# Where the weight operands stand in SBUF, relative to what streams past them

## The chip, the cores and the metric

One core of a Trainium2 chip runs the kernel. The metric is the device time of one execution in microseconds (us). On-chip memory is SBUF (128 partitions) and PSUM, where matmul results land. TensorE does matmuls in two kinds of instruction that the profile shows apart: PEld loads a weight operand into the array, PE streams the other operand (the moving one) past it. PEld of the next matmul runs beside PE of the present one. DVE and ACT are the engines for elementwise work, POOL and SP mostly start DMAs.

## The reference

Two layers, each: a gated feed-forward block (SwiGLU, inner width 2816), a mixer of three branches (RWKV-7, gated linear attention, attention into a memory of 256 rows) that are gated and merged, and a second feed-forward block. 512 tokens, width 1024, float32.

```python
for l in range(DEPTH):
    x = x + 0.5 * swiglu_ffn(rmsnorm(x, ffn1_norm[l]), ffn1_w_in[l], ffn1_w_out[l])
    h = rmsnorm(x, mix_norm[l])
    u_rwkv, u_gla, u_xa, u_gate = split_cols(h @ w_in[l], ...)
    ...
    merged = jnp.einsum('bsjc,jcd,bsjd->bsd', branches, w_branch[l], gates)
    x = x + merged @ w_out[l]
    x = x + 0.5 * swiglu_ffn(rmsnorm(x, ffn2_norm[l]), ffn2_w_in[l], ffn2_w_out[l])
return rmsnorm(x, final_norm)
```

## The kernel before

Every large product runs in the type float32r, on operands that are split in two: `hi` is the value rounded by ACT to float32r, `lo` is the rest, subtracted by DVE (`split`, L721). A product is then three matmuls: the moving hi and the moving lo past the weight's hi, and the moving hi past the weight's lo.

The feed-forward blocks and the mixer's last product cut each product into seven smaller ones (`seven`, L897, a Strassen-like scheme on blocks). A job of `seven` has seven parts, each with a weight of its own, four from two-chunk pieces and three from narrow ones; `part` (L841) runs one part: per 128 rows the two matmuls past hi, and then the ones past lo. All these matmuls stream 256 columns (128x256 in the profile). There are 10,708 of them. The mixer's projections (`proj`, `product`, `mm3`) and the first few columns of each feed-forward block (`whole`, L985) stream 512 columns (128x512); there are about 4,060 of those. About 1,530 float32 matmuls in the mixer are smaller.

`piece` (L834) makes the split weight of one or two parts. A raw tile with two chunks (`wraw`, `q`) goes to tiles `whi`/`wlo` in the pool `wp`; a narrow one, with one chunk (`e[:, 0:1]`, `e[:, 1:2]`, `d`), goes to tiles `fhi`/`flo` in the pool of the stage (`ffn`, or `mg` in the mixer's last product). Each of these four names is a ring of two buffers. In a profile, `hi` and `lo` are the names of all of them.

The moving operands stand in the pool `keep` (`xhi`, `xlo`, `n`, `t`, `yh`, `yl`) or in the pool of the stage (`mh`, `ml`, `xrh`, `xrl`). SBUF is given out pool after pool: `const`, `keep`, `wp`, `nrm`, and then the pool of the stage. Modulo 256 bytes that gives, in the built program:

| operands | pool | byte modulo 256 |
|---|---|---|
| moving xhi, xlo, n, t, yh, yl | keep | 128 |
| moving mh, ml, xrh, xrl | ffn, mg | 192 |
| weights of pieces with two chunks, and of `wide` | wp | 128 |
| weights of narrow pieces | ffn, mg | 192 |

So the distance of a weight from what streams past it (weight minus moving, modulo 256) is 0, 64 or 192, by the part. In the up-projection (moving from `keep`) parts with two-chunk pieces have 0 and narrow ones 64; in the down-projection (moving from `ffn`) two-chunk pieces have 192 and narrow ones 0. The mixer's 512-wide products have 0, those of `whole` 192.

Nothing here is issued in the order of the code: all operations are recorded, a planner (`plan`, `run`, `choose`) simulates the engines with a table of costs, and the program is issued in the order that it found. The planner knows that a buffer of a ring can be written again only when all instructions on the tile that held it before are done. All instructions have the one line of the recorder's call (L316), so the profile is read by tiles.

Of the kernel before, what the change touches and what calls it, by code (L numbers as in the profile page):

```python
# [11 lines left out]
F32 = mybir.dt.float32  # L12
F32R = mybir.dt.float32r
# [6 lines left out]
P = 128  # L20
T = 512
# [7 lines left out]
HALVES = slice(0, H), slice(H, T)  # L29
NWHOLE = [[4, 4], [4, 4]]  # L30
NWARM = 12
NQ = 5
EPS = 1e-6
LN_EPS = 64e-5
# [63 lines left out]
class Tile:  # L98
    def __init__(self, pool, shape, dt, name, tag, bufs):
        self.pool, self.shape, self.dt, self.name, self.tag, self.bufs = pool, shape, dt, name, tag, bufs  # L100
        self.real, self.users, self.writes, self.reads, self.runs = None, [], [], [], ([], [])
        self.before, self.gone, self.free = (), None, False
# [491 lines left out]
class Net:  # L594
    def __init__(self, ctx, tc, I):
        self.nc, self.I = Recorder(tc), I
        self.const = self.pool("const", 1)
        self.keep = self.pool("keep", 1)
        self.wp = self.pool("wp", 2)
        self.nrm = self.pool("nrm", 1)  # L600
        self.psb = self.pool("psb", 3, space=PSUM)
        self.pss = self.pool("pss", 1, space=PSUM)
        self.psy = self.pool("psy", 1, space=PSUM)
        self.dram = self.pool("dram", 1, space=bass.MemoryType.DRAM)
# [24 lines left out]
    def setup(self):  # L629
        nc, I = self.nc, self.I  # L630
        self.pars = [self.const.tile([P, NPAR], F32, name=f"par{l}", tag=f"par{l}") for l in range(L)]
        self.par = self.pars[0]
        nc.scalar.dma_start(out=self.par, in_=I["par"][0])
        self.one = self.const.tile([P, 1], F32, name="one", tag="one")
        nc.vector.memset(self.one, 1.0)
        ps = self.psy.tile([P, T], F32, name="ps_y", tag="y", free=True)
        for _ in range(NWARM):
            nc.tensor.matmul(ps[:, :P], self.one.to_broadcast([P, P]), self.one.to_broadcast([P, P]), start=True, stop=True)
        self.turn = 0
        self.xs = self.keep.tile([P, KD, T], F32, name="x", tag="x")  # L640
        self.x = [self.xs[:, k, :] for k in range(KD)]
        for k in range(KD):
            nc.sync.dma_start(out=self.x[k], in_=I["x"][k * P:(k + 1) * P, :])
        self.cst = self.const.tile([P, P], F32, name="cst", tag="cst")
        nc.sync.dma_start(out=self.cst, in_=I["cst"][:, :P])
        for l in range(1, L):
            nc.sync.dma_start(out=self.pars[l], in_=I["par"][l])
        self.eps = self.const.tile([P, 2], F32, name="eps", tag="eps")
        nc.vector.memset(self.eps[:, 0:1], EPS)
        nc.vector.memset(self.eps[:, 1:2], LN_EPS)  # L650

        self.sums, self.par7 = {}, False
        self.yd = self.dram.tile([3, P, T], F32, name="yd", tag="yd")
        self.yx = self.dram.tile([4, P, T], F32, name="yx", tag="yx")
        self.xd = self.dram.tile([KD, P, T], F32, name="xd", tag="xd")
        self.vd = [self.dram.tile([4, P, T], F32, name=f"vd{l}", tag=f"vd{l}") for l in range(L)]
# [127 lines left out]
    def raw_in(self, pool, norm):  # L784

        hi, lo = (pool.tile([P, 7, T], F32R, name="xr" + c, tag=f"m01{c}", bufs=1) for c in "hl")
        r = pool.tile([P, 2, T], F32R, name="xr", tag="q", bufs=NQ)
        xs = [(hi[:, k, :], lo[:, k, :]) for k in range(7)] + [(r[:, 0], r[:, 1])]
# [44 lines left out]

    def piece(self, pool, raw):  # L834

        p, tags = (self.wp, ("whi", "wlo")) if raw.shape[1] == 2 else (pool, ("fhi", "flo"))
        hi, lo = (p.tile(list(raw.shape), F32R, name=t[1:], tag=t, bufs=2) for t in tags)
        self.split(hi, lo, raw)
        return [(hi[:, c, :], lo[:, c, :]) for c in range(raw.shape[1])]

# [56 lines left out]
    def seven(self, pool, src, n, ops, evict, clear=False):  # L897
# [7 lines left out]
        def begin():  # L905
# [3 lines left out]
            nc.gpsimd.dma_start(out=a[:, 1], in_=w[:, 3], accum_op=ALU.add)  # L909
            q = ring("q", NQ)  # L910
            nc.sync.dma_start(out=q[:, 1], in_=w[:, 2])
            e = ring("q", NQ)
            nc.sync.dma_start(out=e[:, 0], in_=w[:, 1])
# [871 lines left out]
    def mem_norm(self, pool):  # L1785

        nc, I = self.nc, self.I
        mt = [pool.tile([P, 4, NMEM], F32, name="m", tag="q", bufs=NQ) for _ in range(2)]
        mt = [t[:, k, :] for t in mt for k in range(4)]
# [118 lines left out]
```

## Time and profile before

| | |
|---|---|
| median of 3 runs | 2533.76 us (2532.69 to 2534.31) |
| the profiled execution | 2534.68 us |
| its span on the core | 2532.7 us |
| DMA over the span | 358.02 MB, mean 141 GB/s |
| ACT, POOL busy | 1466.9 us (58%), 241.2 us (10%) |

The profile's page gives busy times, the chain of work that ended last and the costliest groups. The timeline view lists instructions in order of their start (start, length, engine, output tile<-moving tile,weight tile, count). A matmul's listed length contains its way through the array, so it is longer than the distance from its start to the start of the next; this distance is what a matmul costs where PE never waits. Below, "distance" means this, start to start.

### The profile page before, as it was taken

To read this page: it belongs to the slowest core of one execution; us is meant where nothing else is said; L and a number is where in the kernel's file an instruction comes from. 1 tells how busy PE (TensorE), PEld (TensorE's weight loads), DVE (VectorE), ACT (ScalarE), POOL (GpSimd) and SP (SyncE) were. 2 spreads that over 40 slices of the span, in tenths; PEclk is the share of its full clock that TensorE was granted. 3 is DMA by queue.
4 is the path that set the end of the run, shared out by engine and by line. 5 is a ranking of instruction groups with operands and counts; after the bars stand their busy time and mean duration, and the time that the engine had idled before them with its cause. 6 is when DMAs were issued, how large, how long until landed. Compare 5 with 4: busy or idle time off the path is not lost.

```text
span 2532.7 us, 47197 instructions
## 1 busy us (share of the span) xinstructions
PE 2506.4 (99%) x17636; PEld 2270.3 (90%) x17636; DVE 2100.5 (83%) x4218; ACT 1466.9 (58%) x2660; POOL 241.2 (10%) x362
## 2 busy tenths in 40 slices
PE   9999999999999999999999999999999999999998
PEld 8999988888788799999989999887887888899998
DVE  8988885778888689888899888866888877898878
ACT  6665666564544456565665656664745444565655
POOL 1111100000000001111112111000000000011110
PEclk9999999999999999999999999999999999999999
DMA  7777762422222456877558777523222225468774
GB/s 199 194 197 189 165 190 76 125 73 69 70 83 74 141 159 150 204 186 184 143 143 203 187 184 170 176 88 101 84 72 88 67 77 171 134 162 205 188 180 105
DMA packets 163668, 358.02 MB, mean 141 GB/s; under 512 B 18256, under 2 KB 38160, under 8 KB 163440
## 3 DMA queue, kind: packets, MB, share of 16 engines
q1 hardware_dynamic: 125344, 288.87, 37.8%
q0 software_dynamic: 36864, 65.03, 16.2%
q8 instruction: 139, 2.28, 0.4%
q10 hardware_dynamic: 1232, 1.11, 0.1%
q14 instruction: 89, 0.73, 0.1%
HBM read 342.88 MB, written 12.06 MB: 140 GB/s over the span
## 4 chain that ended last, share of the span: by engine, by line
PE 85%; DVE 8%; DMA 3%; ACT 2%; issue 2%; SPq 0%; DVEq 0%; ACTq 0%; POOLq 0%
PE ps_b L316 40%; PE ps_i L316 25%; PE ps_f L316 10%; PE ps_c L316 9%; PE ps_y L316 1%; DVE wlo L316 1%; DVE lo L316 1%; DVE x L316 1%; DMA q<-in_ffn_out_dram 1%; ACT whi L316 1%; DMA wraw<-in_w_out_dram 0%; DVE ml L316 0%; DMA wraw<-in_ffn_in_dram 0%; ACT hi L316 0%; DMA q<-in_ffn_in_dram 0%
## 5 line engine op out<-in xcount | busy, mean ns | idle before, releaser
L316 ACT ACTIVATE hi<-q 128x512 fp32r<-128x512 f32 (+3 forms) x384 | 288.9, 756 | 204.8 <-PE ps_i L316 69.6
L316 DVE TENSOR_TENSOR lo<-q,hi 128x512 fp32r<-128x512 f32 (+3 forms) x384 | 321.6, 840 | 43.5 <-ACT hi L316 43.1
L316 PE MATMUL ps_b<-xhi,whi 128*128 128x512 f32 (+1 forms) x880 | 353.7, 402 | 0.2 <-DVE rk_r L316 0.2
L316 PE MATMUL ps_b<-xlo,whi 128*128 128x512 f32 (+1 forms) x880 | 352.9, 401 | 0.1
L316 PE MATMUL ps_b<-xhi,wlo 128*128 128x512 f32 x864 | 347.2, 402 | 0.6 <-DVE wlo L316 0.6
L316 DVE TENSOR_TENSOR wlo<-wraw,whi 128x1024 fp32r<-128x1024 f32 (+1 forms) x172 | 183.7, 1069 | 75.2 <-ACT whi L316 71.0
L316 ACT ACTIVATE whi<-wraw 128x1024 fp32r<-128x1024 f32 (+1 forms) x174 | 161.7, 929 | 130.0 <-PE ps_b L316 100.1
L316 DVE TENSOR_TENSOR lo<-wraw,hi 128x1024 fp32r<-128x1024 f32 (+2 forms) x162 | 191.5, 1182 | 48.5 <-ACT hi L316 46.5
L316 ACT ACTIVATE hi<-wraw 128x1024 fp32r<-128x1024 f32 (+2 forms) x162 | 166.3, 1026 | 106.1 <-PE ps_i L316 41.0
L316 PEld LDWEIGHTS ps_b<-xlo,whi 128*128 128x128 f32 (+1 forms) x880 | 164.1, 187 | 35.6 <-DVE xlo L316 2.5
L316 PEld LDWEIGHTS ps_b<-xhi,whi 128*128 128x128 f32 (+1 forms) x880 | 164.4, 187 | 33.6 <-issue 1.2
L316 PEld LDWEIGHTS ps_b<-xhi,wlo 128*128 128x128 f32 x864 | 162.7, 188 | 32.9 <-DVE wlo L316 2.4
L316 PE MATMUL ps_i<-mh,hi 128*128 128x256 f32 x628 | 157.1, 283 | 4.3 <-ACT hi L316 2.6
L316 PE MATMUL ps_i<-ml,hi 128*128 128x256 f32 x624 | 154.8, 281 | 0.0
L316 PE MATMUL ps_b<-xlo,hi 128*128 128x256 f32 x576 | 144.3, 283 | 0.0
L316 PE MATMUL ps_b<-xhi,hi 128*128 128x256 f32 x576 | 144.3, 283 | 0.0
L316 PEld LDWEIGHTS ps_i<-mh,hi 128*128 128x128 f32 x628 | 119.1, 190 | 5.9 <-ACT hi L316 3.2
L316 PEld LDWEIGHTS ps_i<-ml,hi 128*128 128x128 f32 x624 | 118.1, 190 | 0.0
L316 PEld LDWEIGHTS ps_b<-xhi,hi 128*128 128x128 f32 x576 | 110.5, 192 | 0.2
L316 PEld LDWEIGHTS ps_b<-xlo,hi 128*128 128x128 f32 x576 | 110.4, 192 | 0.2
L316 DVE TENSOR_TENSOR q<-q 128x512 f32<-128x512 f32 (+1 forms) x128 | 85.5, 668 | 22.9 <-DMA q<-in_ffn_in_dram 19.0
L316 ACT ACT_TABLE_LOAD x71 | 91.1, 1283 | 18.9 <-DVE gc L316 10.8
(416 smaller groups left out, 7021.4 us busy)
## 6 DMA issues: line engine op xcount, KB each, us to landing
wraw<-in_w_main_dram SPq DMA_DIRECT2D x108, 512.0 KB, 3.6
wraw<-in_ffn_in_dram SPq DMA_DIRECT2D x102, 512.0 KB, 4.6
q<-in_ffn_in_dram SPq DMA_DIRECT2D x144, 256.0 KB, 4.5
d<-in_ffn_in_dram SPq DMA_DIRECT2D x72, 256.0 KB, 4.2
q<-in_ffn_in_dram POOLq DMA_DIRECT2D x72, 256.0 KB, 6.0
wraw<-in_ffn_in_dram POOLq DMA_DIRECT2D x72, 256.0 KB, 5.2
wraw<-in_ffn_out_dram SPq DMA_DIRECT2D x32, 512.0 KB, 4.4
q<-in_ffn_out_dram SPq DMA_DIRECT2D x64, 256.0 KB, 3.7
```

Source lines behind the costliest of these rows:

```text
L316: return getattr(getattr(self.tc.nc, engine), what)(*(f(v) for v in a), **{n: f(v) for n, v in k.items()})
```

## The change

A tile of 48 floats (192 bytes) in a pool of its own, between `keep` and `wp`, moves `wp` and everything behind it by 192 bytes. A narrow piece no longer has a tile for hi and one for lo, but one tile `hl` of 64 + 2 x 512 floats, in which hi begins at 192 bytes and lo 2048 bytes behind it.

```diff
+SHIFT = 48
...
         self.keep = self.pool("keep", 1)
+        self.shift = self.pool("shift", 1)
         self.wp = self.pool("wp", 2)
...
+        nc.gpsimd.memset(self.shift.tile([P, SHIFT], F32, name="shift", tag="shift"), 0.0)
...
     def piece(self, pool, raw):
 
-        p, tags = (self.wp, ("whi", "wlo")) if raw.shape[1] == 2 else (pool, ("fhi", "flo"))
-        hi, lo = (p.tile(list(raw.shape), F32R, name=t[1:], tag=t, bufs=2) for t in tags)
+        if raw.shape[1] == 2:
+            hi, lo = (self.wp.tile(list(raw.shape), F32R, name=t[1:], tag=t, bufs=2) for t in ("whi", "wlo"))
+        else:
+            n = raw.shape[2]
+            f = pool.tile([P, 64 + 2 * T], F32R, name="hl", tag="fhl", bufs=2)
+            hi, lo = (f[:, SHIFT + i * T:SHIFT + i * T + n].rearrange("p (c t) -> p c t", c=1) for i in range(2))
         self.split(hi, lo, raw)
```

In the built program the moving operands now stand at 128 (`keep` and `ffn`, `mg` alike) and all split weights of these products at 64: the distance is 192 for 10,599 of the pairs of neighbouring 256-wide matmuls (before: 0 for 5,589, 64 for 2,587, 192 for 2,489) and for 3,580 of the 512-wide ones (before: 0 for 2,896, 192 for 776).

The shared tile also changes what the planner knows: hi and lo of a narrow piece come free together, when the last matmul past lo is done, where hi came free a few matmuls earlier. The table of costs is the same, but the planned order moves with it. ACT in the up-projection of the first feed-forward block, before; `fm<-ps`, `ft<-ft` and `mh<-fm` belong to the results of the running job, `hi<-q` are the two narrow pieces `e`, and `hi<-q 128x1024` is the two-chunk piece of the next job:

```order
L316 ACTIVATE fm<-ps_c 128x256
L316 ACTIVATE hi<-q 128x512 x2
L316 ACTIVATE ft<-ft 128x256
L316 ACTIVATE mh<-fm 128x256 x2
L316 ACTIVATE ft<-ps_i 128x256
L316 ACTIVATE hi<-q 128x1024
```

The same engine at the same place of a job, now:

```order
L317 ACTIVATE fm<-ps_c 128x256
L317 ACTIVATE hl<-q 128x512
L317 ACTIVATE ft<-ft 128x256
L317 ACTIVATE hl<-q 128x512
L317 ACTIVATE mh<-fm 128x256 x2
L317 ACTIVATE ft<-ps_i 128x256
```

The rounding of the second narrow piece stands behind the job's Silu (`ft<-ft`) instead of ahead of it. DVE at the same place of a job, before (`lo<-q` 128x512 are the two narrow pieces, `ft<-ps_f` and the two `fm` are results of the job):

```order
L316 TENSOR_TENSOR lo<-wraw,hi 128x1024
L316 TENSOR_TENSOR lo<-q,hi 128x512
L316 TENSOR_TENSOR ft<-ps_f,ft 128x256
L316 SCALAR_TENSOR_TENSOR fm<-ps_i,ft 128x256
L316 TENSOR_TENSOR lo<-q,hi 128x512
L316 SCALAR_TENSOR_TENSOR fm<-fm,ft 128x256
```

DVE there, now:

```order
L317 TENSOR_TENSOR lo<-wraw,hi 128x1024
L317 TENSOR_TENSOR ft<-ps_f,ft 128x256
L317 TENSOR_TENSOR hl<-q,hl 128x512
L317 SCALAR_TENSOR_TENSOR fm<-fm,ft 128x256
L317 SCALAR_TENSOR_TENSOR fm<-ps_i,ft 128x256
L317 TENSOR_TENSOR s_2271<-fm 128x256
L317 TENSOR_TENSOR hl<-q,hl 128x512
```

Both subtractions of narrow pieces moved behind one or two results of the running job. The first matmul past a narrow piece still waits for ACT's hi alone, and the first one past its lo for DVE. The number of instructions is the same but for one memset of POOL at the start.

## The prediction

> **What bounds the kernel now.** I read the page first, then the groups by shape, then the timeline of PE.
>
> ```profile
> span 2532.7 us, 47197 instructions
> PE 2506.4 (99%) x17636; PEld 2270.3 (90%) x17636; DVE 2100.5 (83%) x4218; ACT 1466.9 (58%) x2660; POOL 241.2 (10%) x362
> PEclk9999999999999999999999999999999999999999
> PE 85%; DVE 8%; DMA 3%; ACT 2%; issue 2%; SPq 0%; DVEq 0%; ACTq 0%; POOLq 0%
> ```
>
> PE is busy for 99% of the span, holds 85% of the chain that ended last, and its granted clock is full in all 40 slices. So the kernel is bound by the rate at which PE starts matmuls, and the only thing that the change can win is a shorter distance between starts. The groups say where the distance differs:
>
> ```profile
> L316 PE MATMUL ps_b<-xhi,hi 128*128 128x256 f32 x576 | 144.3, 283 | 0.0
> L316 PE MATMUL ps_i<-t,hi 128*128 128x256 f32 x576 | 79.7, 281 | 0.6 <-ACT ft L316 0.6
> L316 PE MATMUL ps_b<-mh,hi 128*128 128x256 f32 x416 | 100.6, 278 | 0.0
> ```
>
> These are the same matmuls in shape. The first has its weight at distance 0 from what streams, the second at 64, the third at 192, and the means fall from 283 to 281 to 278 ns. Addresses do go with time. The timeline shows what is behind the means. At distance 0:
>
> ```profile
> 303.56 0.28 PE L316 MATMUL ps_b<-xhi,hi 128*128 128x256 f32 x1
> ...
> 305.00 1.12 PE L316 MATMUL ps_f<-n,hi 128*128 128x256 f32 x8
> ```
>
> Twelve matmuls lie between these starts (eight past hi, four past lo): 1.44 us / 12 = 120.0 ns. At distance 192, 48 matmuls in a row:
>
> ```profile
> 2143.58 0.28 PE L316 MATMUL ps_b<-mh,hi 128*128 128x256 f32 x1
> ...
> 2149.23 0.32 PE L316 MATMUL ps_i<-ml,hi 128*128 128x256 f32 x1
> ```
>
> 5.65 us / 48 = 117.7 ns. And once more distance 192, around a stall:
>
> ```profile
> 318.99 0.28 PE L316 MATMUL ps_b<-ml,hi 128*128 128x256 f32 x1
> ...
> 320.01 0.28 PE L316 MATMUL ps_b<-mh,lo 128*128 128x256 f32 x1
> 320.13 0.39 PE L316 MATMUL ps_i<-mh,hi 128*128 128x256 f32 x1
> 320.36 0.40 PE L316 MATMUL ps_b<-mh,lo 128*128 128x256 f32 x2
> 320.59 0.28 PE L316 MATMUL ps_b<-mh,hi 128*128 128x256 f32 x1
> ...
> 322.36 0.40 PE L316 MATMUL ps_f<-mh,lo 128*128 128x256 f32 x2
> ```
>
> Ahead of the stall nine steps take 1.02 us, 113.3 ns each. Behind it fifteen steps take 1.77 us, 118.0 ns each, with the same tiles at the same addresses. So the distance in bytes does not fix the beat. At 192 there are two beats that hold themselves, 113.3 and 117.7 ns, and which one runs is inherited from how the stretch began.
>
> How does a stretch get into the quick beat? From a settled stretch at distance 0:
>
> ```profile
> 900.51 0.28 PE L316 MATMUL ps_i<-mh,hi 128*128 128x256 f32 x1
> ...
> 901.95 0.28 PE L316 MATMUL ps_i<-mh,hi 128*128 128x256 f32 x1
> 902.07 0.28 PE L316 MATMUL ps_i<-ml,hi 128*128 128x256 f32 x1
> ...
> 903.42 0.28 PE L316 MATMUL ps_b<-ml,hi 128*128 128x256 f32 x1
> ```
>
> Narrow pieces, at 0: twelve steps in 1.44 us (120.0 ns); then a two-chunk piece, at 192: twelve steps in 1.35 us (112.5 ns, with 10 ns of rounding at each end). Over the whole trace, 16 stalls end in a stretch of at least seven steps at 192 between 256-wide matmuls: fifteen go on at 117.7 ns, one (at 129.85 us) at 113.3. I found no stretch at 192 that went from 117.7 to 113.3 without the address distance changing.
>
> **The change part by part.** The sum is made against the profiled execution, 2534.68 us, which is 0.92 us above the median of the runs shown, 2533.76.
>
> *256-wide matmuls.* I counted the start-to-start distances of the timeline by the address distance of each pair, leaving out pairs with a stall (over 132 ns). Distance 0: 5,544 pairs, mean 119.7. Distance 64: 2,583 pairs, mean 117.4. Distance 192: 2,464 pairs, mean 115.3, a mixture of the two beats. Together 10,591 pairs, 1,250.8 us, mean 118.1. Now nearly all are at 192. The settled stretches at distance 0 that led into the quick beat are gone, so I take the beat that follows a stall: 117.7. That gives 5,544 x 2.0 = 11.1 us won, 2,583 x 0.3 = 0.8 us and 2,464 x 2.4 = 5.9 us lost: 4.4 us won. One stall in 16 led to the quick beat; if 1 in 16 of all pairs runs there, another 10,591 / 16 x 4.4 ns = 2.9 us is won. The bounds are all pairs at 117.7 (4.4 us) and all at 113.3 (10,591 x 4.8 ns = 50.8 us). I take 7.3 us, near the lower end, because fifteen of sixteen restarts stand there.
>
> *512-wide matmuls.* They are about 2,570 pairs without a stall at distance 0, and these have two values too:
>
> ```profile
> 458.01 35.61 PE ps_b L316 x157
> ```
>
> ```profile
> 458.07 0.39 PE L316 MATMUL ps_b<-xhi,wlo 128*128 128x512 f32 x1
> ...
> 459.23 0.39 PE L316 MATMUL ps_b<-xlo,whi 128*128 128x512 f32 x1
> 37.05 0.39 PE L316 MATMUL ps_b<-xrl,hi 128*128 128x512 f32 x1
> ...
> 40.72 0.39 PE L316 MATMUL ps_i<-xrh,lo 128*128 128x512 f32 x1
> ```
>
> The row of the chain is a long stretch at distance 0: 35.61 / 157 = 226.8 ns. The next two, of the timeline, are its beginning behind a wait: five steps in 1.16 us, 232.0 ns, before it settles. The mean over all is 229.3. The last two are at 192: sixteen steps in 3.67 us, 229.4 (229.0 over all 748 pairs without a stall). So 192 has neither the bad beginning nor the good end: 2,570 x 0.3 = 0.8 us won. The bounds are 226.8 (6.4 us won) and 232.0 (6.9 us lost). I take the measured middle since `whole` runs 192 in this very program.
>
> *The shared tile.* ACT may write the hi of a narrow piece only when the matmuls past lo of the piece two before are done, four matmuls later than now.
>
> ```profile
> 297.63 0.63 ACT L316 ACTIVATE hi<-q 128x512 fp32r<-128x512 f32 x1
> 299.00 0.63 ACT L316 ACTIVATE hi<-q 128x512 fp32r<-128x512 f32 x1 [0.73 <-PE ps_i L316]
> 303.62 0.62 ACT L316 ACTIVATE hi<-d 128x512 fp32r<-128x512 f32 x1
> 298.80 0.64 PE L316 MATMUL ps_i<-xhi,lo 128*128 128x256 f32 x4
> 302.15 1.11 PE L316 MATMUL ps_i<-t,hi 128*128 128x256 f32 x8
> 306.44 0.28 PE L316 MATMUL ps_c<-xhi,hi 128*128 128x256 f32 x1
> 307.85 0.28 PE L316 MATMUL ps_i<-xhi,hi 128*128 128x256 f32 x1
> ```
>
> The rounding at 299.00 started when PE had left hi of `ps_i<-xhi,hi`; the four matmuls past lo run from 298.80 to 299.44. So it will start 0.44 us later, and Silu now stands ahead of it. It ends at 299.63 and is first used at 306.44, 6.8 us later; the piece at 297.63 ends at 298.26 for 302.15 (3.9 us), `d` at 304.24 for 307.85 (3.6 us). 0.44 us hides in each of these. Behind the waiting rounding on ACT stand results of the job, for which DVE and then PE wait; all 384 narrow pieces with 0.44 us exposed would be 169 us, none is 0. I take 0.
>
> ```profile
> PE ps_i L316 <- ACT hi L316: 2.6, 3, 1.2
> ```
>
> ```profile
> 975.00:1235.00 260.00, 260.00 (x2197) 259.89 (x2197) 229.03 (x419) 160.05 (x293) 45.97 (x54) 1.00 0.78 185
> 2230.00:2275.00 45.00, 45.00 (x380) 44.92 (x379) 44.83 (x86) 33.24 (x66) 6.90 (x8) 1.00 0.72 175
> ```
>
> The first row is PE's total wait for such a write: 2.6 us. The two stretches (span, then PE, PEld, DVE, ACT, POOL busy) say what is late next: DVE is busy for 229.0 of 260 us in a feed-forward block, and for 44.8 of 45 us at the start of one.
>
> *The rest.* The memset is one instruction of POOL, which is busy for 10% of the span: 0. The float32 matmuls of the mixer move by 64 bytes against each other here and there; no row separates that, and I take 0.
>
> Sum: 7.3 + 0.8 = 8.1 us. 2534.7 - 8.1 = 2526.6 for the profiled execution, and 2525.7 for the median.
>
> [...]
>
> **The rivals.**
>
> *The quick beat holds everywhere.* If the 113.3 beat is what 192 gives and the 117.7 after stalls is left over from the neighbours at 0 and 64, all 10,591 pairs come to 113.3: 50.8 us. For it: 192 has the lowest mean, and only there did long stretches at 113.3 appear. Against it: fifteen of sixteen restarts. DVE at 88% of a block, and saturated at its start, would give some back: 2534.7 - 50.8 + about 6 = 2489.7, or 2489 for the median.
>
> *The beat goes with the stage, not with the address.* The three address distances sit in different parts with different tiles; then nothing but the order moves: 2533.8, within 3 us. For it: at one distance, 192, both beats occur. Against it: at 900-903 us the same kind of moving tiles changes beat when the piece changes place. [...]
>
> *DVE and ACT come late.* The second narrow piece is now rounded and subtracted behind results of the job, 0.44 us later, on a DVE that is full at 2230-2275. If one in ten of the 384 pieces exposes 0.44 us, that is 16.9 us against the 8.1 won: 2534.7 + 8.8 = 2543.5, 2542.6 for the median, slower. From 18 exposed pieces on (8.1 / 0.44) the change loses, from 30 on by over 0.2%. Against it: leads of 3.6 to 6.8 us.
>
> **How the numbers follow.** 0.2% of the time (5.1 us) is about what a measurement of this kernel can tell from no change: faster means below 2528.7, slower above 2538.8. My forecast, 2525.7, has a chance of 0.57; with its 512-wide term at either end and 0 to 25% of the pairs in the quick beat its own range is 2514 to 2532. About 0.4 of the 0.57 lies below 2528.7. The quick beat everywhere has 0.15, no effect of the address 0.16, late DVE and ACT 0.12. Faster: 0.40 + 0.15 + 0.02 = 0.57; same: 0.17 + 0.14 = 0.31; slower: 0.12. The range reaches to 2489 and 2542; what lies outside is half of the first rival and half of the last.
>
> **What would show it.** In the profile after, the groups that read 283 should read 279 to 281, and `ps_b<-mh,hi` should rise from 278 to about 279: the forecast. Steps of 113.3 ns throughout and means well below 278 would show the quick beat everywhere; 283 left in groups now at 192 would show that the address is not the cause. The 512-wide steps of the mixer should be 229 in long stretches, where 226.8 stands now. Rows where PE waits for `hl`, or more than a few us of them in the waits, would show the last rival. The forecast is wrong if stretches at 192 find the quick beat by themselves after a stall.

## The result, and the profile after

| | before | after |
|---|---|---|
| median | 2532.9 us (8 runs, 2531.51 to 2534.31) | 2525.88 us (8 runs, 2523.99 to 2529.64) |
| the profiled execution | 2534.68 us | 2527.03 us |

The ratio is 0.9972, with a 95% interval from 0.9962 to 0.9983: 0.28% faster, 7.0 us between the medians. The forecast was 2525.7 us, 8.1 us won.

The page of after: span, busy times, granted clock in 40 slices, and the chain by engine:

```profile
span 2524.8 us, 47193 instructions
PE 2500.3 (99%) x17636; PEld 2262.6 (90%) x17636; DVE 2101.2 (83%) x4218; ACT 1473.8 (58%) x2660; POOL 242.0 (10%) x363
PEclk9999999999999999999999999999999999999999
PE 85%; DVE 9%; DMA 3%; issue 1%; ACT 1%; SPq 0%; DVEq 0%; POOL 0%; POOLq 0%; ACTq 0%
```

Nothing changed in kind. PE is busy for 99% of the span at a full granted clock and holds 85% of the chain. The span is 7.9 us shorter with the same matmuls. The groups by shape:

```profile
L317 PE MATMUL ps_b<-xhi,hi 128*128 128x256 f32 x576 | 141.6, 279 | 0.0
L317 PE MATMUL ps_i<-t,hl 128*128 128x256 f32 x864 | 113.0, 279 | 0.0
L317 PE MATMUL ps_b<-mh,hi 128*128 128x256 f32 x416 | 101.8, 279 | 0.0
```

These are the groups that read 283, 281 and 278 ns (hi and lo of `t` share a name now). All three read 279. The timeline, first in the middle of a stretch, then behind a wait:

```profile
1140.06 0.28 PE L317 MATMUL ps_c<-mh,hl 128*128 128x256 f32 x1
...
1142.88 0.28 PE L317 MATMUL ps_i<-mh,hi 128*128 128x256 f32 x1
...
1498.73 0.28 PE L317 MATMUL ps_b<-mh,hi 128*128 128x256 f32 x1
...
1499.64 0.62 PE L317 MATMUL ps_b<-mh,lo 128*128 128x256 f32 x4
1500.41 0.36 PE L317 MATMUL ps_i<-mh,hl 128*128 128x256 f32 x1 [0.15 <-DVE x L317]
1500.60 0.28 PE L317 MATMUL ps_i<-ml,hl 128*128 128x256 f32 x1
...
1501.85 0.28 PE L317 MATMUL ps_b<-xhi,hi 128*128 128x256 f32 x1
```

From 1140.06 to 1142.88 lie 24 steps: 117.5 ns, the slower of the two beats at distance 192. The longest stretches like this run for 750 to 1,037 matmuls. The second place is one of the few in the quick beat: eight steps in 0.91 us (113.8), a wait of 0.15 us, and eleven steps in 1.25 us (113.6). There are 43 places where a stretch of at least eight steps at 192 begins, 37 behind a stall and six behind a 512-wide or smaller matmul without one. At 40 it went on at 117.7 and at three (two stalls, one 512-wide matmul) at 113.3; about 850 of 10,594 steps (8%) were quick. So the sign that the prediction named for its being wrong, the quick beat behind a stall, did appear, twice in 37. One of the two is the place shown, where the stretch ahead of the stall was quick already.

The chain's long stretch of 512 columns, which took 35.61 us before, and PE's waits for the shared tile:

```profile
453.78 35.95 PE ps_b L317 x157
```

```profile
PE ps_i L317 <- ACT hl L317: 0.4, 1, 0.4
```

35.95 / 157 = 229.0 ns instead of 226.8. The shared tile made PE wait once, for 0.4 us.

Counted over the whole trace (start to start, stalls over 132 ns left out; a pair's distance is that of the next matmul's weight from what streams in the present one), a 256-wide step takes 117.43 ns on the mean instead of 118.10. Over 10,591 steps that is 7.1 us. The 512-wide ones went the other way: 229.25 ns (2,569 at 229.31, 748 at 229.04) became 229.79 (3,240 at distance 192 at 229.70, 84 at 64 at 233.19), 1.8 us lost.

### The profile page after: what moved, and what is told of

The parts are those of the page before. It is cut to its first block, busy times and chain, and to the rows that moved or that the text cites. A ratio compares the mean times of both kernels' runs of the same rounds, so it can differ in the third digit from the quotient of the medians.

```text
span 2524.8 us, 47193 instructions
## 1 busy us (share of the span) xinstructions
PE 2500.3 (99%) x17636; PEld 2262.6 (90%) x17636; DVE 2101.2 (83%) x4218; ACT 1473.8 (58%) x2660; POOL 242.0 (10%) x363
## 4 chain that ended last, share of the span: by engine, by line
PE 85%; DVE 9%; DMA 3%; issue 1%; ACT 1%; SPq 0%; DVEq 0%; POOL 0%; POOLq 0%; ACTq 0%
PE ps_b L317 41%; PE ps_i L317 25%; PE ps_f L317 10%; PE ps_c L317 8%; PE ps_y L317 2%; DVE ml L317 1%; DVE wlo L317 1%; DMA wraw<-in_ffn_in_dram 1%; DVE x L317 1%; DVE hl L317 1%; DVE lo L317 1%; DMA q<-in_ffn_out_dram 1%; DMA wraw<-in_w_out_dram 1%; DVE s L317 1%; DVE q L317 1%
## 5 line engine op out<-in xcount | busy, mean ns | idle before, releaser
L317 ACT ACTIVATE hl<-q 128x512 fp32r<-128x512 f32 (+1 forms) x256 | 158.4, 619 | 134.3 <-PE ps_i L317 39.7
L317 DVE TENSOR_TENSOR hl<-q,hl 128x512 fp32r<-128x512 f32 (+1 forms) x256 | 171.3, 670 | 10.5 <-ACT hl L317 9.8
L317 ACT ACTIVATE hi<-q 128x1024 fp32r<-128x1024 f32 (+1 forms) x128 | 132.1, 1032 | 77.8 <-PE ps_b L317 57.7
L317 DVE TENSOR_TENSOR lo<-q,hi 128x1024 fp32r<-128x1024 f32 (+1 forms) x128 | 152.3, 1190 | 25.7 <-ACT hi L317 25.2
L317 PE MATMUL ps_i<-mh,hl 128*128 128x256 f32 x832 | 166.6, 281 | 2.0 <-DVE x L317 1.5
L317 PEld LDWEIGHTS ps_i<-mh,hl 128*128 128x128 f32 x832 | 134.7, 188 | 3.6 <-issue 1.4
L317 ACT ACTIVATE hl<-d 128x512 fp32r<-128x512 f32 (+1 forms) x128 | 79.1, 618 | 59.7 <-PE ps_i L317 35.5
L317 PE MATMUL ps_i<-xhi,hl 128*128 128x256 f32 x576 | 113.0, 279 | 0.0
L317 PE MATMUL ps_i<-t,hl 128*128 128x256 f32 x864 | 113.0, 279 | 0.0
```

What stands on the lines that cost most here:

```text
L317: return getattr(getattr(self.tc.nc, engine), what)(*(f(v) for v in a), **{n: f(v) for n, v in k.items()})
```

## The experiments

Each was run beside the kernel before on one chip; ratios are to that. The medians of before were 2532.9 us beside the change and 2530.1 to 2531.5 us beside the others, so rows are compared by their ratios, and medians of different rows only within some 3 us.

| kernel | median | ratio, 95% interval | 256-wide step | quick steps | stall excess |
|---|---|---|---|---|---|
| before | 2532.9 | | 118.10 ns | 15% | 12.0 us |
| after | 2525.88 | 0.9972 [0.9962, 0.9983] | 117.43 | 8% | 10.5 |
| shared tile alone | 2529.59 | 0.9997 [0.9988, 1.0006] | 117.99 | 17% | 9.1 |
| shift alone | 2517.97 | 0.9949 [0.9936, 0.9961] | 116.42 | 46% | 12.8 |
| all at 0 | 2546.22 | 1.0061 [1.0047, 1.0075] | 119.97 | 0% | 7.5 |
| narrow at 64 | 2503.35 | 0.9894 [0.9881, 0.9908] | 114.14 | 81% | 26.8 |
| narrow at 64, real pace | 2494.2 | 0.9855 [0.9838, 0.9871] | 113.65 | 93% | 14.9 |
| after, real pace | 2530.52 | 0.9995 [0.9986, 1.0004] | 117.76 | 0.3% | 10.7 |

The step is the mean without stalls in the profiled execution; a quick step is one of at most 115 ns with neighbours of at most 115. The stall excess is what the steps over 132 ns took beyond the mean of their class.

**The shift alone.** Narrow pieces keep their two tiles, so they stay at distance 0; two-chunk pieces and the mixer go to 192.

```diff
-        if raw.shape[1] == 2:
...
-            f = pool.tile([P, 64 + 2 * T], F32R, name="hl", tag="fhl", bufs=2)
-            hi, lo = (f[:, SHIFT + i * T:SHIFT + i * T + n].rearrange("p (c t) -> p c t", c=1) for i in range(2))
+        p, tags = (self.wp, ("whi", "wlo")) if raw.shape[1] == 2 else (pool, ("fhi", "flo"))
+        hi, lo = (p.tile(list(raw.shape), F32R, name=t[1:], tag=t, bufs=2) for t in tags)
```

> The shift alone; the narrow pieces keep two tiles of their own and stand at distance 0, the two-chunk pieces (up and down) and the mixer at 192. Pairs of 256 columns: 6,160 at 192 and 4,533 at 0. Inherited beat (my theory): a settled stretch at 0 (119.7 ns) sends the stretch at 192 behind it into 113.3, so the mean is at best (6,160 x 113.3 + 4,533 x 119.7) / 10,693 = 116.0 against 117.4 in the changed kernel: 15 us faster than it, about 2511 us; with the mixture that the kernel before shows at 192 (115.3) still 3 us faster, about 2523 us. Address alone (every distance has one beat, 117.4 at 192 and 119.7 at 0): 10 us slower than the changed kernel, about 2536 us. Address without any effect: as the changed kernel, 2526 us.

2517.97 us, between the 2511 and 2523 us of my theory. It is 0.51% faster than before, where the change is 0.28% faster, with fewer steps at 192 and 4,483 at 0, the slowest of the three distances (119.7 ns in the kernel before). Groups by shape, a two-chunk piece and a narrow one:

```profile
L317 PE MATMUL ps_b<-xhi,hi 128*128 128x256 f32 x576 | 137.9, 276 | 0.0
L317 PE MATMUL ps_i<-t,hi 128*128 128x256 f32 x576 | 80.9, 283 | 0.0
```

The first stands at 192 and reads 276 ns, where the changed kernel has the same distance and reads 279. Its timeline, a narrow piece and then a two-chunk one:

```profile
1147.99 0.28 PE L317 MATMUL ps_i<-mh,hi 128*128 128x256 f32 x1
...
1149.43 0.28 PE L317 MATMUL ps_i<-mh,hi 128*128 128x256 f32 x1
...
1150.22 0.28 PE L317 MATMUL ps_i<-ml,hi 128*128 128x256 f32 x1
```

Twelve steps in 1.44 us (120.0 ns) at 0, then seven in 0.79 us (113) at 192. Over the trace, 6,097 steps at 192 have a mean of 114.2 ns and 4,483 at 0 one of 119.5. Address alone had forecast 2536 us; it is out. Of 236 stretches of at least six steps at 192 right behind one at 0 that had settled near 120 ns, 228 were quick. The full 113.3 was not reached, in part because at 24 of the 26 places where a stretch at 192 begins behind a stall or another kind of matmul it went on at 117.7 until the next piece at 0.

**The shared tile alone.** The change without its spare pool, and hi at the start of the shared tile.

```diff
-SHIFT = 48
+SHIFT = 0
-        self.shift = self.pool("shift", 1)
-        nc.gpsimd.memset(self.shift.tile([P, SHIFT], F32, name="shift", tag="shift"), 0.0)
```

> The shared tile for narrow pieces alone, hi at its start and nothing shifted: the addresses modulo 256 are those of the kernel before, the planner's order and the later release of hi are those of the change. Theory (the shared tile costs and wins nothing, the address does it all): 2532.9 us, within 2 us of the kernel before. Rival, the order or the shared tile is what won: 2526 us. Rival, the shared tile costs something that the address then more than paid back: above 2536 us.

No difference: the ratio's interval, 0.9988 to 1.0006, allows from 3 us won to 1.5 us lost. The group of `ps_b<-xhi,hi` reads 283 ns again:

```profile
L317 PE MATMUL ps_b<-xhi,hi 128*128 128x256 f32 x576 | 144.3, 283 | 0.0
```

The later release of hi and the new order cost nothing that can be measured, so what the change won came with the addresses.

**Bare streams.** 48 matmuls into one PSUM tile, weights at a chosen distance from the moving tiles, each stream behind a wait for ACT.

```diff
+            for i in range(count):
+                q = 0 if i == count - 1 else i % 8
+                d = ds[i // each]
+                w = (move + d) % 64 + P * (i % 12)
+                nc.tensor.matmul(ps[:, :n], wt[:, w:w + P], mv[:, q * T + move:q * T + move + n], start=i == 0,
+                                 stop=i == count - 1, skip_group_check=True)
```

> Nothing is computed of the reference here: streams of 48 float32r matmuls into one PSUM tile, each behind a stall, with all other engines idle (in some with VectorE busy), at eight distances for 256 columns and four for 512, and with a change of distance in the middle, four times over. Inherited beat (my theory): behind a stall 192 gives 117.7 ns in at least 14 of 16 streams and 113.3 in the rest; 0 gives 120.0; 64 gives 117.7; the second half of a stream that goes from 0 to 192 runs at 113.3. 512 columns: 0 begins at 232 and settles at 226.7, 192 keeps 229. Address alone: each distance has one value in all its streams, whatever came ahead, and 0 then 192 gives 117.4 in its second half. [...] Neighbours (the beats come from the load of the other engines on SBUF): the streams with VectorE busy differ from the others by more than 2 ns.

The timeline, one row for a stream; in this order: 0 throughout, 192 throughout, 224 throughout, 0 then 192, 64 (in the quick beat) then 192, 192 then 64; and of 512 columns 0, 64 and 192:

```profile
274.22 6.01 PE L317 MATMUL ps_b<-mv,wt 128*128 128x256 f32 x48 [0.57 <-ACT mv L317]
313.43 5.92 PE L317 MATMUL ps_b<-mv,wt 128*128 128x256 f32 x48 [0.56 <-ACT mv L317]
319.92 5.86 PE L317 MATMUL ps_b<-mv,wt 128*128 128x256 f32 x48 [0.56 <-ACT mv L317]
438.71 5.86 PE L317 MATMUL ps_b<-mv,wt 128*128 128x256 f32 x48 [0.56 <-ACT mv L317]
458.00 5.73 PE L317 MATMUL ps_b<-mv,wt 128*128 128x256 f32 x48 [0.56 <-ACT mv L317]
490.30 5.81 PE L317 MATMUL ps_b<-mv,wt 128*128 128x256 f32 x48 [0.56 <-ACT mv L317]
...
339.33 11.22 PE L317 MATMUL ps_b<-mv,wt 128*128 128x512 f32 x48 [0.55 <-ACT mv L317]
363.91 11.46 PE L317 MATMUL ps_b<-mv,wt 128*128 128x512 f32 x48 [0.55 <-ACT mv L317]
413.81 11.28 PE L317 MATMUL ps_b<-mv,wt 128*128 128x512 f32 x48 [0.55 <-ACT mv L317]
```

A row's length less 0.28 us (the last matmul's own) over 47 is the mean step, with the first step of about 0.22 us in it: 121.9, 120.0, 118.7, 118.7, 116.0 and 117.7 ns. The steps by themselves:

| 256 columns, distance | behind a stall | in the second half of a stream |
|---|---|---|
| 0 | settles at 120.0 within some fifteen steps, always | 120.0, whatever came ahead |
| 192 | 117.8, always | 113.3 behind 0 (4 of 4) and behind a quick 64 (4 of 4); 117.8 behind 128 (4 of 4) |
| 64 | 117.8 or 113.3 | 117.8 behind 0 (4 of 4); 113.3 behind 192 (4 of 4) and behind 128 (4 of 4) |
| 128 | 118.4 to 120.0 | 118.3 to 118.9 |
| 224 | settles at 116.7 (4 of 4) | 116.6 behind a quick 64 (6 of 6, in the later streams) |

At 0 and at 192 the same distance gave the same step with the moving tiles at 0, 128 or 192, so it is the difference that counts. With VectorE busy on eight additions during the stream (5.5 of 6.0 us) nothing changed (117.8 at 192, 120.0 at 0). The beats come with the other engines idle (in 6 us of such a stream at 0, DVE and POOL 0.00 us, ACT 0.17), depend on the difference of the two addresses, and are inherited (113.3 at 192 behind 0, 117.8 behind a stall): address alone and neighbours are out, and so is an address without any effect, with 120.0 at 0 against 117.8 at 192. One step of mine was wrong: 64 behind a stall isn't fixed to 117.7.

**All at 0, the control.** The same spare pool behind the pools of the weights, and narrow pieces in two tiles, as in the kernel before. The diff shows the pools, against the change.

```diff
         self.keep = self.pool("keep", 1)
-        self.shift = self.pool("shift", 1)
         self.wp = self.pool("wp", 2)
         self.nrm = self.pool("nrm", 1)
+        self.shift = self.pool("shift", 1)
```

> The control: the same spare pool of 192 bytes, but placed behind the pools of the weights, and narrow pieces in two tiles as before, so that weights and moving operands both start at 128 (modulo 256): distance 0 everywhere, 10,693 pairs of 256 columns and 3,715 of 512. The distance decides (inherited beat or address alone): every settled stretch runs at 120.0, mean 119.7 against 118.1 in the kernel before: 10,591 x 1.6 ns = 17 us slower than the kernel before, about 2548 us; 512 columns as before (229.3). The pool or the order decides, not the distance: 2526 to 2533 us.

2546.22 us, against about 2548 expected: 0.61% slower than before by the same 192 bytes at another place. In the built programs this kernel, the shift alone and the kernel before have the same order of instructions on PE, DVE and SP, so the order is not what sets them apart. Modulo 512 the pairs fall into 5,564 at 0 and 5,064 at 256, both with a mean of 120.0 ns, so modulo 256 is enough here. The group of down-projection matmuls that read 278 before:

```profile
L317 PE MATMUL ps_b<-mh,hi 128*128 128x256 f32 x416 | 103.9, 283 | 0.0
```

**Narrow pieces at 64.** In the bare streams 64 behind 192 ran at 113.3, and 192 behind a quick 64 as well. So the changed kernel with one number altered:

```diff
-            hi, lo = (f[:, SHIFT + i * T:SHIFT + i * T + n].rearrange("p (c t) -> p c t", c=1) for i in range(2))
+            hi, lo = (f[:, 16 + i * T:16 + i * T + n].rearrange("p (c t) -> p c t", c=1) for i in range(2))
```

> The changed kernel with the narrow pieces 64 bytes into their shared tile instead of 192: two-chunk pieces (6,160 pairs) stay at distance 192, narrow ones (4,463 pairs) stand at 64. Inherited beat, with the steps that the bare streams showed (192 behind a stall 117.8; 64 behind a 192 at 117.8 runs at 113.3; 192 behind a 64 at 113.3 runs at 113.3): after each stall at most one piece at 117.7, then 113.3 until the next stall, a mean near 113.8 against 117.4 in the changed kernel: 10,541 x 3.6 ns = 38 us won, of which VectorE, which is busy for 44.8 of 45 us at the start of a feed-forward block, may take back some 6: 2488 to 2496 us. Address alone (192 always 117.4, 64 always 117.4 as the kernel before has them): 2526 us. A later release or VectorE decides (PE faster, but waiting): above 2505 us with PE waiting on DVE for tens of us more.

2503.35 us, 1.06% faster than before, and 7 us above what I expected. The beats came nearly as forecast (mean 114.14 against 113.8): 6,075 steps at 192 have a mean of 114.3 ns, 4,347 at 64 one of 113.9. Of the stretches of at least six steps at 192 right behind one at 64, 203 of 203 were quick where the one at 64 was, and 2 of 22 where it was slow; here too the beat is inherited. But 189 steps were stalls, with an excess of 26.8 us instead of 10.5. In the groups they hide in part in the mean:

```profile
L317 PE MATMUL ps_b<-xhi,hi 128*128 128x256 f32 x576 | 138.2, 276 | 0.0
L317 PE MATMUL ps_i<-mh,hl 128*128 128x256 f32 x832 | 165.1, 281 | 2.4 <-DVE x L317 1.6
```

In the quick beat without a stall the second would read 276 like the first. Five more nanoseconds over 832 are 4.2 us, and they come on top of the 2.4 us that the page shows as idle time ahead: 46 of these matmuls waited inside their listed length, 3.3 us in all, and most others above 276 ran in the slow beat. I had allowed for late work at one place (6 us); the stalls were spread over the jobs of all feed-forward blocks. (The profiled execution, 2507.63 us, is the slowest of its runs, 4.3 us above the median, so the counts may be somewhat above those of the median run.)

**More bare streams.** Among others, four parts of twelve matmuls that alternate between two distances, 64 and 192 behind seven lengths of stall, and 512 columns at eight distances.

> Nothing is computed of the reference here: bare streams again, 512 columns at eight distances behind a stall, in three lengths of the operation ahead of them, and with a change of distance; 256 columns at 64 and 192 behind seven lengths of stall; and streams of four parts that alternate 192 and 64, 64 and 192, 0 and 192, 224 and 64, 192 and 96. Inherited beat: 192, 64, 192, 64 runs 117.7 in its first part and 113.3 in all others; 64, 192, 64, 192 runs 113.3 at the latest from its third part; the beat at 64 or 192 behind a stall may differ between lengths of the stall (117.7 or 113.3), but only between these two. 512 columns: 0 first 235, then 226.7; 64 and 128 233; 192 229; a distance that beats 0 over the first ten steps would be below 231. Address alone: no stream changes its beat without changing its distance, and 192 has the same beat in every part.

Timeline rows of 192, 64, 192, 64 with two lengths of the wait, of 64, 192, 64, 192, and of 192 and 96 in turn:

```profile
363.78 5.76 PE L317 MATMUL ps_b<-mv,wt 128*128 128x256 f32 x48 [0.41 <-ACT mv L317]
370.00 5.88 PE L317 MATMUL ps_b<-mv,wt 128*128 128x256 f32 x48 [0.46 <-ACT mv L317]
382.60 5.73 PE L317 MATMUL ps_b<-mv,wt 128*128 128x256 f32 x48 [0.41 <-ACT mv L317]
458.45 5.95 PE L317 MATMUL ps_b<-mv,wt 128*128 128x256 f32 x48 [0.41 <-ACT mv L317]
```

The first went 117.7, 113.3, 113.3, 113.3. The second took two changes longer: 117.9, 117.9, 117.6, 113.4. Of six such streams three did the one and three the other; all six were quick in the fourth part. So "113.3 in all others" held in three of six. 64, 192, 64, 192 was quick from its first part in all six streams, 192 and 96 in turn never. Behind a stall 64 was quick in 8 of 14 single streams, 192 in none of 14. No settled beat changed in the middle of a part. For 512 columns 0 settles at 226.7, 192 keeps 229.0, and the six other distances stay between 231.9 and 234.3.

**The real pace.** With narrow pieces at 64, the planner still ordered VectorE's and ScalarE's work for matmuls of 120.4 ns.

```diff
-                o.busy = n / 2.4 + 13.7
+                o.busy = n / 2.4 + {256: 7.0, 512: 16.3}.get(n, 13.7)
```

> The kernel with two-chunk pieces at 192 and narrow ones at 64 again, and the planner told the pace that it then has: 113.7 ns for a matmul of 256 columns instead of 120.4, 229.6 for 512 instead of 227.0 (due times of VectorE's and ScalarE's work follow from these). In that kernel 177 stalled pairs of 256 columns held 25 us, against about 10 in the changed kernel. Order theory (the work of VectorE and ScalarE came late because it was ordered for a slower PE): the stalls fall to about 12 us, 2489 to 2495 us. Throughput theory (VectorE has no time left at those places, whatever the order): stalls stay at 20 us or more, 2500 to 2507 us. The beats themselves stay as they are, 113.3 in most stretches, by either.

2494.2 us, 1.45% faster than before and the best kernel of the study. 63 stalls with 14.9 us are left, 11.9 us less than in the kernel planned for 120.4 ns, so the order theory holds. The stalls aren't all of it: with fewer of them the quick beat covers 93% of the steps instead of 81%, and 0.49 ns less over some 10,500 steps is 5 us. The page:

```profile
L317 PE MATMUL ps_i<-mh,hl 128*128 128x256 f32 x832 | 160.5, 277 | 2.3 <-DVE x L317 2.0
L317 PE MATMUL ps_i<-t,hl 128*128 128x256 f32 x864 | 109.9, 276 | 0.0
```

281 fell to 277; 276 is what 113.3 ns looks like in this column.

**The pace alone, as a control.** The changed kernel, planned for the 117.5 and 229.6 ns that it has.

```diff
-                o.busy = n / 2.4 + 13.7
+                o.busy = n / 2.4 + {256: 10.8, 512: 16.3}.get(n, 13.7)
```

> The changed kernel with nothing altered but the planner's figures, set to the pace that it has: 117.5 ns for 256 columns instead of 120.4, 229.6 for 512 instead of 227.0. It is the control for the kernel with the real pace at 192 and 64. If the gain there (9 us) came from stalls that only the faster beat had brought, nothing is to be had here: the changed kernel has some 10.5 us of stalls between matmuls of 256 columns, and stays at 2523 to 2529 us. If the planner's figures were worth 9 us by themselves, it comes to about 2517 us.

2530.52 us, which neither theory had: by the ratios 0.23% above the changed kernel, and 5.4 us between the profiled executions, though its 10.7 us of stalls are the same. The planner's figures were not worth 9 us. Most of what it lost are the quick steps: 30 instead of 850. Its mean step is 117.76 ns against 117.43, and 0.33 x 10,559 = 3.5 us. In this execution the quick beat came at one of 24 places where a stretch of at least eight steps at 192 begins, and the next stall came soon. The rest of the loss, some 2 us in steps between 512-wide and smaller matmuls, I did not follow up.

## Why the prediction was right, step by step

**256-wide matmuls: 7.3 us forecast, 7.1 measured.** The mechanism held. The beat after a stall is 117.7: 35 of 37 in the changed kernel, all 64 bare streams that began at 192. Of the 82 quick stretches of six or more steps at 192 in the kernel before, 81 began behind a distance 0, and with those gone they became rare; "the shift alone" keeps them and is by the ratios 0.23%, some 6 us, faster than the change. I allowed 1 in 16 steps (2.9 us) for the quick beat, and 1 in 12.5 came (850 x 4.4 ns = 3.7 us); the rest was 3.4 us where I had 4.4. That agreement is luck in good part: the 850 lie in four stretches, one of them of about 580 steps, and the control with another order had almost none. I counted 1 in 16 stalls and applied it to steps, although one stretch can last from 10 to 1,000 of them. This part may be what spreads the times from 2524 to 2530; only one execution has a trace.

**512-wide matmuls: 0.8 us won forecast, 1.8 lost measured.** This step failed, in its sign. I took 229.0 for 192 from `whole`, where 486 of 735 steps are the 24th or later behind a stall. In the mixer some 870 of 2,505 steps are among the first three behind one, and they take 231.4 at 192, not 229. "Neither the bad beginning nor the good end" was half right: at 0 the beginning is 231.9, so 192 saves 0.5 ns there, and it loses 2.3 ns on every step once 0 would have settled. With 84 steps at 64 that I had left out (233.2), the loss lies inside the bounds of 6.9.

**The shared tile: 0 forecast.** Right within 3 us by its own run, and one wait of 0.4 us in the trace of after. The leads of 3.6 to 6.8 us covered the 0.44 us.

**Sum.** First to last start of a matmul fell by 7.9 us: 7.1 won, 1.8 lost, about 2.9 less in stalls of these two kinds, and 0.3 more elsewhere. I had forecast nothing for stalls; the total came close by luck, because this made up for the 512-wide step. The forecast's "own range", 2514 to 2532, does not follow from the terms that it names: 0 to 25% of the pairs quick (4.4 to 16.1 us won) and the 512-wide term at either end (6.4 won, 6.9 lost) give 2511 to 2536 us. The result lies inside both.

**The rivals.** *The quick beat everywhere* is what the bare streams exclude for 192 alone (117.8 behind every stall); it comes with 192 and 64 in turn. *The beat goes with the stage* falls with the two kernels that move addresses alone, with the same order on PE: 2518 and 2546 us, where an address without any effect would have left both at the time of before. *Late DVE and ACT* did not come with this change, but with the kernel that has the faster beat: 16 us more of stalls, of which 12 went when the planner knew the pace; so most came from an order planned for a slower PE rather than from a tile.

Open: what makes the beats, why 64 goes into one or the other behind a stall, and why 192 nearly always goes into the slow one. The length of the stall may play a part for 64: five of seven lengths gave the same beat both times. But behind the other two it was quick once and slow once, so it isn't this length alone.

## What to carry to other kernels

Where PE is always busy and streams short rows (here 256 columns), compare start-to-start distances of one shape by where the weight and the moving operand stand (modulo 256): the same matmuls took 1.7% less time at the best placing tried than at the worst (2503.35 against 2546.22 us). Don't give each distance one price: a beat may be inherited (here 113.3 or 117.7 ns at 192), so measure pairs of neighbours, and behind stalls, before giving all operands the distance that has the best mean. When the bound engine becomes faster, tell the planner, or the others come late (1.06% became 1.45%); where it had not become much faster, as in the changed kernel, the true pace won nothing.

## What the runs showed of the hardware

The mean at 192 in the kernel before, 115.3 ns, was the best of the three distances because 0 stood next to it; given to every operand, 192 runs at 117.4. For 256 columns of float32r three beats hold themselves at full clock at 0, 64 and 192: 113.3, 117.7 and 120.0 ns. Other distances have others: 224 settled at 116.7 in all bare streams with that distance alone, quicker than 192 behind a stall (117.8) without needing a neighbour. No kernel here was run with it. A change from 192 to 64 turned the slow beat into the quick one in 7 of 10 bare streams at the first change, without any stall. A step of 129 ns, too short to count as a stall here, did it once in the changed kernel, at 1490.56 us.
